# Second product of an MLP on one core: who reads PSUM, and who makes the lower parts of the stationary operands

## The chip, the cores and the metric

The program runs on one core of one Trainium2 chip. The metric is the device time of one execution in microseconds (us). Three runs of the kernel before gave 2746.65, 2749.07 and 2749.72 us; the median, 2749.07 us, is the time before.

The engines are called as in the profile: PE (TensorE, matrix products), PEld (its weight loads), DVE (VectorE), ACT (ScalarE), POOL (GpSimd) and SP (SyncE, which issues most DMAs). Each works through its own queue in order. PE writes its products to PSUM; DVE and ACT read PSUM, and POOL works on SBUF alone in this kernel.

## The reference

One block of a network: two mixers (a long convolution and a gated linear attention), a projection, and an MLP. The change is in the MLP, of which this is the part that matters:

```python
def _sq_relu_mlp(h, w1, w2):
    return jnp.square(jax.nn.relu(h @ w1)) @ w2
...
        x = x + g1 * (jnp.concatenate([y_hy_l, y_gla_l], axis=-1) @ w_out[l])
        h2 = _rms_norm(x, norm_mlp[l]) * (1.0 + sc2) + sh2
        x = x + g2 * _sq_relu_mlp(h2, w_mlp1[l], w_mlp2[l])
...
    return _rms_norm(x, norm_final)
```

Here `x` is 2048 x 1024, `w_mlp1` 1024 x 4096 and `w_mlp2` 4096 x 1024, all float32.

## The kernel before

Both products of the MLP are done with a scheme of seven block products in place of eight (Strassen's, in Winograd's form). Each operand is cut into 2 x 2 blocks, sums of blocks make seven left and seven right operands, and the seven products are added into the four blocks of the result, some of them by continuing in the same PSUM bank. To keep float32 accuracy, each operand is split into an upper part (`hi`, a cast to float32r by ACT) and a lower part (`lo` = operand - `hi`), and each block product is hi*hi + hi*lo + lo*hi: three matmuls for one.

**The first product** runs in two halves of the tokens (`tb` 0 and 1). For each pair of 128 columns `n` it leaves four blocks of squared ReLU outputs and three sums of them (`s1`, `s2`, `s4`; `put`, lines 1385 to 1407) in the DRAM tensor `d_m`. In the second half `n` runs down from 15 to 0, so that the last block that is put is `tb` 1, `n` 0. The sums `s1` and `s2` are made by POOL, the other two by DVE.

**The second product** (lines 1535 to 1653) is where the change works. It has 64 units: for each of 8 quarters `g` of the inner dimension (two blocks of 256 of the 4096 each) it walks over 8 token blocks `t` of 256 tokens. In the tables of this text "unit t of quarter g" is one pass of the loop `for at, (g, t) in enumerate(un)`. The result of all tokens stays in SBUF as `acc` (16 tiles of 128 x 1024, which begin as the residual `x1`).

One unit has seven block products of six matmuls each, called m1 to m7 after their number in the table `PR`. Each matmul is 128x128 by 128x512. PE's order in a unit is m1, m2, then m4 of the unit before ("late4"), m6, m3 of the unit before ("late3"), m5, m7. Three PSUM banks serve a unit: `x` takes m1, then m6, m7 and m4 on top of it, `y` takes m5 and then m3, `z` takes m2. After every product the bank's present sum is added to a block of `acc` (`more`). So PE can't begin m6 before the bank `x` has been read after m1; it can't begin m7 before it has been read after m6, nor late4 before it has been read after m7. Two products (2.7 us of matmuls) lie between in each case.

Seven such reads belong to a unit. Four of them are "direct": DVE adds PSUM to `acc` (line 1575). The other three (m2, late4, late3) go through ACT, which copies PSUM to `tmp` (line 1578), and POOL, which adds `tmp` to `acc` (line 1579).

The stationary operands `u` of a unit come by one DMA of 896 KB (`load_u`, line 1545) into one of two buffers `ur`, and are split operand by operand (`split_u`): ACT casts `uh`, DVE subtracts for `ul` (helper `split`, lines 231 and 232). `uh` and `ul` have one buffer for each of the seven operands, so that the operand of unit t+1 can be made only after PE has used that of unit t; it is needed about one unit later. Operands 4 and 3 are made in their own unit, after late4 and late3 of the unit before. The DMA for unit t+2 waits until the last operand of unit t (number 3) has been split.

Once per quarter the moving operands change. In unit 7 of a quarter and unit 0 of the next `w2_split` makes them: 14 casts `wh` by ACT and 14 subtractions `wl` by DVE (128x512), with 4 sums of blocks on POOL (`sum_b`, lines 1245 and 1247). In unit 1 of each quarter `w2_raw` loads the next two blocks of `w2` (2 DMAs of 1 MB) and lets POOL multiply them by the gate (8 multiplications of 128x512, line 1442) and make four first differences (lines 1443 and 1444).

In the last quarter (g = 7) each unit also finishes the tokens of the unit before: ACT squares (`squares`), POOL makes the factor, DVE scales with `nf` (`finish`, line 1602), and a DMA writes the output.

The framework's scheduler decides the order in which the instructions stand on each engine within small limits; on PE it is the order of the code.

Of the kernel before, what the change touches and what calls it, by code (L numbers as in the profile page):

```python
# [10 lines left out]
F32 = mybir.dt.float32  # L11
# [3 lines left out]
ALU = mybir.AluOpType  # L15
# [3 lines left out]
P = 128  # L19
# [191 lines left out]
def hybrid_block(ctx: ExitStack, tc, a, out, dbg=None):  # L211
    nc = tc.nc
# [5 lines left out]
    dve = nc.vector  # L218
    gps = nc.gpsimd
# [10 lines left out]
    def split(hi, lo, src):  # L230
        nc.scalar.copy(hi, src)  # L231
        dve.tensor_sub(lo, src, hi.bitcast(F32))  # L232
# [20 lines left out]
    def pt(name="ps"):  # L253
        return psp.tile([P, 512], F32, tag="ps", bufs=8, name=name)

    def sb(name, side="left", stack=ctx):
        return stack.enter_context(tc.tile_pool(name=name, bufs=1, side=side, reuse_waits="tile"))
# [971 lines left out]
    PR = {1: (0, 0), 2: (1, 1), 3: (6, 2), 4: (2, 6), 5: (4, 4), 6: (5, 5), 7: (3, 3)}  # L1229
# [48 lines left out]
    with ExitStack() as eo:  # L1278
        op = sb("op", stack=eo)
# [95 lines left out]
    def full(ps, w, m, start):  # L1375
        for kp in range(4):
            prod(ps, w, m, kp, start and kp == 0, kp == 3)
# [6 lines left out]
    cs_ = {}  # L1384

    def put(n, tb, i, j, src, add=None):

        tag, bufs = ("c0", 2) if i == j == 0 else ("c1", 2) if i == j else ("c", 5)
        c = us.tile([P, 512], F32, tag=tag, bufs=bufs, name="c")
        if add is None:  # L1390
            act(c[:], src[:], AF.Relu)
        else:
            dve.tensor_add(c[:], src[:], add[:])
            act(c[:], c[:], AF.Relu)
        act(c[:], c[:], AF.Square)
        cs_[n, i, j] = c
        if (i, j) != (0, 1):
            store(n, tb, {(0, 0): 0, (1, 0): 1, (1, 1): 2}[i, j], c)
            return

        s1, s2, s4 = (us.tile([P, 512], F32, tag="c", bufs=5, name=m) for m in ("s1", "s2", "s4"))
        gps.tensor_tensor(s1[:], c[:], cs_[n, 1, 1][:], op=ALU.add)
        gps.tensor_sub(s2[:], s1[:], cs_[n, 0, 0][:])
        dve.tensor_sub(c[:], cs_[n, 0, 0][:], c[:])
        dve.tensor_sub(s4[:], cs_[n, 1, 0][:], s2[:])
        for slot, t in ((3, c), (4, s1), (5, s2), (6, s4)):
            store(n, tb, slot, t)

    def store(n, tb, slot, c):
        (put_out if tb and n < 1 else dma)(d_m[tb, n, :, :, slot, :], c[:].rearrange("p (q t) -> p q t", q=4))  # L1410
# [26 lines left out]
    def w2_raw(n):  # L1437

        r = w2r[n] = raw_tile()
        dma(r[:, 0:4, :], a["w2"][n])  # L1440
        for q in range(4):
            gps.tensor_mul(r[:, q, :], r[:, q, :], g2b[:, (q // 2) * 512:(q // 2 + 1) * 512])
        gps.tensor_sub(r[:, 4, :], r[:, 3, :], r[:, 0, :])
        gps.tensor_sub(r[:, 3, :], r[:, 2, :], r[:, 3, :])
# [13 lines left out]
    for tb in range(2):  # L1458

        late = None  # L1460
# [6 lines left out]
        for at in range(1, 16):  # L1467
            n = ns[at]
            w, nxt = wops, {}
            x, y = pt(), pt()  # L1470
# [20 lines left out]
            z = pt()  # L1491
# [29 lines left out]
            def late4(n=n, x=x, w=w, tb=tb):  # L1521
                full(x, w, 4, False)
                put(n, tb, 1, 0, x)

            def late3(n=n, y=y, w=w, u2=u2, tb=tb):
                full(y, w, 3, False)
                put(n, tb, 0, 1, y, u2)

            late = (late4, late3)
# [8 lines left out]
    mf = sb("mf", stack=em)  # L1538
    w2s, uts, ops = w2s, {}, {}
# [6 lines left out]

    def split_u(at, m):
        hi, lo = (mf.tile([P, 2, P], F32R, tag=f"{t}{m}", bufs=1, name=t) for t in ("uh", "ul"))
        split(hi[:], lo[:], uts[at][:, :, PR[m][0], :])
        ops[at, m] = (hi, lo)  # L1550

    load_u(0)
# [10 lines left out]
    def full2(ps, at, m, start):  # L1563
        hi, lo = ops.pop((at, m))
        for kb in range(2):
            wh, wl = w2s[m, kb]
            for i, (x_, y_) in enumerate(((hi, wh), (hi, wl), (lo, wh))):
                mm(ps[:], x_[:, kb, :], y_[:], start=start and kb + i == 0, stop=kb == 1 and i == 2,  # L1568
                   skip_group_check=True)

    def more(ps, t, i, j, direct):

        ac = acc[2 * t + i][:, j * 512:(j + 1) * 512]
        if direct:
            dve.tensor_add(ac, ac, ps[:])  # L1575
        else:
            tmp = mf.tile([P, 512], F32, tag="tmp", bufs=4, name="tmp")
            nc.scalar.copy(tmp[:], ps[:])  # L1578
            gps.tensor_add(ac, ac, tmp[:])  # L1579

    def refill(at, m):

        if at < len(un):
            if un[at][1] == 0:
                w2_split(un[at][0], m, (0, 1))
            split_u(at, m)

    def squares(t):
        rs_ = []
        for i in range(2):  # L1590
            ss = mf.tile([P, 4], F32, tag="ss", bufs=4, name="ss")
            for j in range(2):
                tmp = mf.tile([P, 512], F32, tag="tmp", bufs=4, name="tmp")
                act(tmp[:], acc[2 * t + i][:, j * 512:(j + 1) * 512], AF.Square, accum_out=ss[:, j:j + 1])  # L1594
            gps.tensor_add(ss[:, 2:3], ss[:, 0:1], ss[:, 1:2])  # L1595
            rs_.append(rstd_of(mf, ss[:, 2:3], 1, 1.0 / D, "mrs"))
        return rs_
# [7 lines left out]
    late = None  # L1605
    for at, (g, t) in enumerate(un):
        if g == 0:
            for i in range(2):
                dma(acc[2 * t + i][:], d_x1[(2 * t + i) * P:(2 * t + i + 1) * P, :])
        if t == 1 and g < 7:  # L1610
            for kb in range(2):
                w2_raw(2 * g + 2 + kb)
        x, y = pt(), pt()
        full2(x, at, 1, True)
        more(x, t, 0, 0, True)
        refill(at + 1, 1)
        z = pt()
        full2(z, at, 2, True)
        more(z, t, 0, 0, False)
        refill(at + 1, 2)  # L1620
        if late:
            late[0](False)
        refill(at, 4)
        full2(x, at, 6, False)
        more(x, t, 0, 1, True)
        refill(at + 1, 6)
        if late:
            late[1](False)
        refill(at, 3)
        rs_ = squares(t - 1) if g == 7 and t else None  # L1630
        full2(y, at, 5, True)
        more(y, t, 1, 1, True)
        refill(at + 1, 5)
        full2(x, at, 7, False)
        more(x, t, 1, 1, True)
        refill(at + 1, 7)
        if rs_:
            finish(t - 1, rs_)
        if at + 2 < len(un):
            load_u(at + 2)  # L1640

        def late4(direct, at=at, x=x, t=t):
            full2(x, at, 4, False)
            more(x, t, 1, 0, direct)

        def late3(direct, at=at, y=y, t=t):
            full2(y, at, 3, False)
            more(y, t, 0, 1, direct)

        late = (late4, late3)  # L1650
    late[0](True)
    late[1](True)
    finish(7, squares(7))


# [16 lines left out]
```

## Time and profile before

| what | value |
| --- | --- |
| median of three runs | 2749.07 us |
| the profiled execution, its time | 2743.28 us |
| its span in the profile | 2741.5 us |
| mean granted TensorE clock | 0.966 |
| first matmul of the second product starts | 1973.71 us |
| last matmuls of the second product | about 2732 us |

The profile shows one execution. Its page lists the busy time of each engine, the chain of work that ended last, and groups of instructions: line, engine, operation, output<-inputs, shape and count, then busy time, mean duration of one in ns, and the idle time of the engine just before these instructions with what ended it. The timeline lists instructions in order of time: start and length in us, engine, line, operation, and in brackets the idle time before it and what ended that. The stage of the second product, from 1973.7 us on, is 28% of the span.

### The profile page before, as it was taken

The page shows a single profiled execution, that of the slowest core. Times are in us where ns is not written, and L with a number is a line of the kernel's source. Part 1 is how long each engine was busy: PE and PEld are TensorE (multiplying, and loading weights), DVE is VectorE, ACT ScalarE, POOL GpSimd, SP SyncE. Part 2 cuts the span into 40 slices and gives each one's busy share as a digit, 9 for nine tenths or more (in the row PEclk, how much of TensorE's full clock was granted, in tenths as well). Part 3 has the DMA queues.
Part 4 walks back from the last instruction along what each step waited for, and adds up shares of the span by engine and source line. Part 5 has one row for each costly group of instructions (what it writes and reads, how often), then busy time and mean ns, then how long its engine had stood idle before and what let it go on. Part 6 is the DMA issues. An engine that isn't in the chain of part 4 may idle for free. (4 is left out here: it accounts for less than half of the span.)

```text
span 2741.5 us, 37947 instructions
## 1 busy us (share of the span) xinstructions
PE 2512.5 (92%) x13320; PEld 2059.1 (75%) x13320; DVE 1774.2 (65%) x2772; ACT 1253.4 (46%) x2453; POOL 1073.9 (39%) x898
## 2 busy tenths in 40 slices
PE   9899999999998888999899999999698888888887
PEld 5678978897886777788688877888576667666665
DVE  5755366726668777624655547555578887887887
ACT  6463342325226464434555555555443443443354
POOL 2130321223112122332344434444656655646555
PEclk9899999999999899899999999999899999999999
DMA  5425344434448776656454545545552323232323
GB/s 190 152 81 171 117 139 139 143 107 130 157 139 219 221 226 162 216 174 198 154 160 140 161 145 162 162 146 154 191 202 101 109 81 112 98 112 81 112 96 148
DMA packets 298974, 405.02 MB, mean 148 GB/s; under 512 B 23700, under 2 KB 223256, under 8 KB 288672
## 3 DMA queue, kind: packets, MB, share of 16 engines
q1 hardware_dynamic: 292208, 392.38, 45.2%
q10 hardware_dynamic: 6576, 10.23, 1.1%
q8 instruction: 105, 1.72, 0.3%
q14 instruction: 85, 0.70, 0.1%
HBM read 271.92 MB, written 130.62 MB: 147 GB/s over the span
## 5 line engine op out<-in xcount | busy, mean ns | idle before, releaser
L1568 PE MATMUL ps<-wh,uh 128*128 128x512 f32 x896 | 367.6, 411 | 112.0 <-DVE acc L1575 94.2
L232 DVE TENSOR_TENSOR ul<-ur,uh 128x256 fp32r<-128x256 f32 x448 | 356.0, 821 | 121.1 <-ACT uh L231 120.8
L232 DVE TENSOR_TENSOR wl<-raw,wh 128x512 fp32r<-128x512 f32 x329 | 340.8, 1052 | 97.5 <-ACT wh L231 97.4
L1579 POOL TENSOR_TENSOR acc<-acc,tmp 128x512 f32<-128x512 f32 x190 | 268.8, 1430 | 278.5 <-DVE ul L232 130.7
L1568 PE MATMUL ps<-wh,ul 128*128 128x512 f32 x896 | 358.0, 400 | 4.3 <-DVE ul L232 4.3
L1568 PE MATMUL ps<-wl,uh 128*128 128x512 f32 x896 | 358.7, 400 | 0.0
L1373 PE MATMUL ps<-bh,wh 128*128 128x512 f32 x896 | 349.9, 392 | 6.6 <-ACT bh L231 2.8
L1373 PE MATMUL ps<-bl,wh 128*128 128x512 f32 x896 | 351.1, 392 | 4.4 <-DVE bl L232 4.3
L1373 PE MATMUL ps<-bh,wl 128*128 128x512 f32 x896 | 349.2, 390 | 2.7 <-DVE wl L232 2.7
L231 ACT CAST uh<-ur 128x256 fp32r<-128x256 f32 x448 | 170.5, 407 | 348.2 <-PE ps L1568 171.0
L1568 PEld LDWEIGHTS ps<-wh,uh 128*128 128x128 f32 x896 | 174.2, 194 | 184.2 <-ACT uh L231 57.7
L231 ACT CAST wh<-raw 128x512 fp32r<-128x512 f32 x329 | 202.5, 622 | 213.0 <-PE ps L1373 169.5
L1568 PEld LDWEIGHTS ps<-wh,ul 128*128 128x128 f32 x896 | 173.7, 194 | 43.3 <-DVE ul L232 5.0
L1373 PEld LDWEIGHTS ps<-bh,wh 128*128 128x128 f32 x896 | 168.8, 189 | 45.6 <-ACT bh L231 5.1
L1373 PEld LDWEIGHTS ps<-bl,wh 128*128 128x128 f32 x896 | 168.9, 189 | 42.8 <-DVE bl L232 8.3
L1568 PEld LDWEIGHTS ps<-wl,uh 128*128 128x128 f32 x896 | 174.5, 195 | 33.8
L1373 PEld LDWEIGHTS ps<-bh,wl 128*128 128x128 f32 x896 | 168.6, 188 | 38.2 <-DVE wl L232 3.5
L1575 DVE TENSOR_TENSOR acc<-acc,ps 128x512 f32<-128x512 f32 x258 | 174.3, 676 | 14.9 <-PE ps L1568 14.8
L226 PE MATMUL ph<-hth,whi 128*128 128x512 f32 x384 | 150.9, 393 | 0.0
L228 PE MATMUL ph<-hth,wlo 128*128 128x512 f32 x384 | 149.6, 390 | 0.0
L227 PE MATMUL ph<-htl,whi 128*128 128x512 f32 x384 | 149.4, 389 | 0.0
L226 PE MATMUL pv<-whi,hth 128*128 128x264 f32 x512 | 146.6, 287 | 2.9 <-ACT whi L231 2.9
(283 smaller groups left out, 5313.2 us busy)
## 6 DMA issues: line engine op xcount, KB each, us to landing
ur<-d_m SPq DMA_DIRECT2D x64, 896.0 KB, 4.8
raw<-in_w_dram SPq DMA_DIRECT2D x47, 1024.0 KB, 5.7
d_m<-c SPq DMA_DIRECT2D x124, 256.0 KB, 2.6
d_m<-s SPq DMA_DIRECT2D x93, 256.0 KB, 3.1
xt<-in_x_dram SPq DMA_DIRECT2D x32, 512.0 KB, 5.2
mwt<-in_wada_dram SPq DMA_DIRECT2D x64, 256.0 KB, 3.0
raw<-in_wi_vg_dram SPq DMA_DIRECT2D x20, 528.0 KB, 4.9
wada<-in_wada_dram SPq DMA_DIRECT2D x16, 512.0 KB, 7.3
```

Source lines behind the costliest of these rows:

```text
L226: mm(ps, lh, rh, start=first, stop=False)
L227: mm(ps, lh, rl, start=False, stop=False)
L228: mm(ps, ll, rh, start=False, stop=last)
L231: nc.scalar.copy(hi, src)
L232: dve.tensor_sub(lo, src, hi.bitcast(F32))
L1373: mm(ps[:], x_[:, sl], y_[:, j, :], start=start and i == 0, stop=stop and i == 2, skip_group_check=True)
L1568: mm(ps[:], x_[:, kb, :], y_[:], start=start and kb + i == 0, stop=kb == 1 and i == 2, skip_group_check=True)
L1575: dve.tensor_add(ac, ac, ps[:])
L1579: gps.tensor_add(ac, ac, tmp[:])
```

## The change

Three things are changed.

1. In the second product all seven reads of PSUM in a unit are additions by DVE straight into `acc`. The copies by ACT and the additions by POOL (190 of each in the profile) are gone, and with them the choice `direct`.
2. The subtractions for `ul` go to POOL, except those of the first unit (`at` 0), which stay on DVE. The casts `uh` stay on ACT. The split of the moving operands (`wh`, `wl`) stays as it was.
3. In the first product the sums `s1` and `s2` of the last block put (`tb` 1, `n` 0) are made by DVE in place of POOL.

```diff
@@ put
         s1, s2, s4 = (us.tile([P, 512], F32, tag="c", bufs=5, name=m) for m in ("s1", "s2", "s4"))
-        gps.tensor_tensor(s1[:], c[:], cs_[n, 1, 1][:], op=ALU.add)
-        gps.tensor_sub(s2[:], s1[:], cs_[n, 0, 0][:])
+        eng = dve if tb and n < 1 else gps
+        eng.tensor_tensor(s1[:], c[:], cs_[n, 1, 1][:], op=ALU.add)
+        eng.tensor_sub(s2[:], s1[:], cs_[n, 0, 0][:])
@@ split_u
-        split(hi[:], lo[:], uts[at][:, :, PR[m][0], :])
+        src = uts[at][:, :, PR[m][0], :]
+        nc.scalar.copy(hi[:], src)
+        (gps if at else dve).tensor_sub(lo[:], src, hi[:].bitcast(F32))
@@ more
-    def more(ps, t, i, j, direct):
+    def more(ps, t, i, j):
 
         ac = acc[2 * t + i][:, j * 512:(j + 1) * 512]
-        if direct:
-            dve.tensor_add(ac, ac, ps[:])
-        else:
-            tmp = mf.tile([P, 512], F32, tag="tmp", bufs=4, name="tmp")
-            nc.scalar.copy(tmp[:], ps[:])
-            gps.tensor_add(ac, ac, tmp[:])
+        dve.tensor_add(ac, ac, ps[:])
```

The calls of `more`, `late4` and `late3` lose the argument `direct` and are otherwise the same. PE's order is unchanged.

**POOL, unit 1 of a quarter.** In the rows below `raw` is a block of `w2`, `g2b` the gate, `ur` the loaded operands of a unit (each number is one unit). Before, POOL's queue around `w2_raw` (lines 1442 to 1444) has the additions of `tmp`:

```order
L1579 TENSOR_TENSOR acc2_17493<-acc2_17493,tmp_22329 128x512
L1442 TENSOR_TENSOR raw_22293<-raw_22293,g2b_17509 128x512 x4
L1579 TENSOR_TENSOR acc1_17492<-acc1_17492,tmp_22342 128x512
L1443 TENSOR_TENSOR raw_22293<-raw_22293 128x512
L1444 TENSOR_TENSOR raw_22293<-raw_22293 128x512
L1579 TENSOR_TENSOR acc0_17491<-acc0_17491,tmp_22366 128x512
L1442 TENSOR_TENSOR raw_22301<-raw_22301,g2b_17509 128x512 x4
L1443 TENSOR_TENSOR raw_22301<-raw_22301 128x512
L1444 TENSOR_TENSOR raw_22301<-raw_22301 128x512
```

Now, at the same place (the lines of `w2_raw` are 1443 to 1445 in the changed file, and `ul` is line 1552), the subtractions stand there. `ur_21903` belongs to unit 1, `ur_22001` to unit 2 and `ur_22099` to unit 3 of the quarter:

```order
L1552 TENSOR_TENSOR ul_22029<-ur_22001,uh_22028 128x256
L1552 TENSOR_TENSOR ul_22041<-ur_22001,uh_22040 128x256
L1552 TENSOR_TENSOR ul_22052<-ur_21903,uh_22051 128x256
L1443 TENSOR_TENSOR raw_22003<-raw_22003,g2b_17509 128x512 x4
L1552 TENSOR_TENSOR ul_22063<-ur_22001,uh_22062 128x256
L1444 TENSOR_TENSOR raw_22003<-raw_22003 128x512
L1552 TENSOR_TENSOR ul_22074<-ur_21903,uh_22073 128x256
L1445 TENSOR_TENSOR raw_22003<-raw_22003 128x512
L1552 TENSOR_TENSOR ul_22085<-ur_22001,uh_22084 128x256
L1443 TENSOR_TENSOR raw_22011<-raw_22011,g2b_17509 128x512 x4
L1552 TENSOR_TENSOR ul_22096<-ur_22001,uh_22095 128x256
L1444 TENSOR_TENSOR raw_22011<-raw_22011 128x512
```

By the order of the code the seven `ul` here are operands 1 and 2 of unit 2, operand 4 of unit 1, then operand 6 of unit 2, 3 of unit 1, 5 and 7 of unit 2. The last one stands behind all eight multiplications; one more difference (line 1445) follows, and then operand 1 of unit 3.

**DVE, the change of quarters.** `wl` is the lower part of a moving operand, `ps` a PSUM bank. Before, from the first `wl` of unit 7 on:

```order
L232 TENSOR_TENSOR wl_22847<-raw_22293,wh_22846 128x512
L1575 TENSOR_TENSOR acc14_17505<-acc14_17505,ps_22837 128x512
L232 TENSOR_TENSOR wl_22852<-raw_22301,wh_22851 128x512
L232 TENSOR_TENSOR ul_22857<-ur_22835,uh_22856 128x256
L232 TENSOR_TENSOR wl_22871<-raw_22293,wh_22870 128x512
L232 TENSOR_TENSOR wl_22876<-raw_22301,wh_22875 128x512
L232 TENSOR_TENSOR ul_22881<-ur_22835,uh_22880 128x256
L232 TENSOR_TENSOR ul_22894<-ur_22747,uh_22893 128x256
L1575 TENSOR_TENSOR acc14_17505<-acc14_17505,ps_22837 128x512
```

Now the same stretch, with line 1577 for the reads of PSUM:

```order
L232 TENSOR_TENSOR wl_22521<-raw_22003,wh_22520 128x512
L1577 TENSOR_TENSOR acc14_17505<-acc14_17505,ps_22511 128x512
L232 TENSOR_TENSOR wl_22526<-raw_22011,wh_22525 128x512
L1577 TENSOR_TENSOR acc14_17505<-acc14_17505,ps_22534 128x512
L232 TENSOR_TENSOR wl_22543<-raw_22003,wh_22542 128x512
L232 TENSOR_TENSOR wl_22548<-raw_22011,wh_22547 128x512
L1577 TENSOR_TENSOR acc13_17504<-acc13_17504,ps_22429 128x512
L1577 TENSOR_TENSOR acc14_17505<-acc14_17505,ps_22511 128x512
```

Between the reads after m1 and after m6 of unit 7 (the first and the last `acc14` row, bank 22837 before and 22511 now) there stood three `wl` and three `ul`; now there stand three `wl` and two further reads, those after m2 and after late4.

More of the change, by code (lines that the diff above doesn't have):

```diff
@@ L1614, in hybrid_block @@
         full2(x, at, 1, True)
-        more(x, t, 0, 0, True)
+        more(x, t, 0, 0)
         refill(at + 1, 1)
@@ L1618, in hybrid_block @@
         full2(z, at, 2, True)
-        more(z, t, 0, 0, False)
+        more(z, t, 0, 0)
         refill(at + 1, 2)
         if late:
-            late[0](False)
+            late[0]()
         refill(at, 4)
         full2(x, at, 6, False)
-        more(x, t, 0, 1, True)
+        more(x, t, 0, 1)
         refill(at + 1, 6)
         if late:
-            late[1](False)
+            late[1]()
         refill(at, 3)
@@ L1631, in hybrid_block @@
         full2(y, at, 5, True)
-        more(y, t, 1, 1, True)
+        more(y, t, 1, 1)
         refill(at + 1, 5)
         full2(x, at, 7, False)
-        more(x, t, 1, 1, True)
+        more(x, t, 1, 1)
         refill(at + 1, 7)
@@ L1640, in hybrid_block, with late4, late3 @@
             load_u(at + 2)
-        def late4(direct, at=at, x=x, t=t):
+        def late4(at=at, x=x, t=t):
             full2(x, at, 4, False)
-            more(x, t, 1, 0, direct)
-        def late3(direct, at=at, y=y, t=t):
+            more(x, t, 1, 0)
+        def late3(at=at, y=y, t=t):
             full2(y, at, 3, False)
-            more(y, t, 0, 1, direct)
+            more(y, t, 0, 1)
         late = (late4, late3)
-    late[0](True)
-    late[1](True)
+    late[0]()
+    late[1]()
     finish(7, squares(7))
```

## The prediction

> **What bounds the kernel now.** I read the page first, for the stage and its waits, then PE's timeline, then DVE's and POOL's at the places where PE stops.
>
> ```profile
> span 2741.5 us, 37947 instructions
> ...
> L1568 PE MATMUL ps<-wh,uh 128*128 128x512 f32 x896 | 367.6, 411 | 112.0 <-DVE acc L1575 94.2
> L232 DVE TENSOR_TENSOR ul<-ur,uh 128x256 fp32r<-128x256 f32 x448 | 356.0, 821 | 121.1 <-ACT uh L231 120.8
> ...
> L1579 POOL TENSOR_TENSOR acc<-acc,tmp 128x512 f32<-128x512 f32 x190 | 268.8, 1430 | 278.5 <-DVE ul L232 130.7
> ...
> L1575 DVE TENSOR_TENSOR acc<-acc,ps 128x512 f32<-128x512 f32 x258 | 174.3, 676 | 14.9 <-PE ps L1568 14.8
> ```
>
> PE waits 94 us for DVE's reads of PSUM, though a read takes only 676 ns. DVE is late because of what stands ahead in its queue: `ul`, 821 ns in the mean. PE's timeline shows what it could do and where it stops.
>
> ```profile
> 2301.21 0.39 PE L1568 MATMUL ps<-wh,ul 128*128 128x512 f32 x1
> 2301.44 0.39 PE L1568 MATMUL ps<-wh,uh 128*128 128x512 f32 x1
> ...
> 2246.47 0.39 PE L1568 MATMUL ps<-wh,ul 128*128 128x512 f32 x1
> 2251.07 0.77 PE L1568 MATMUL ps<-wh,uh 128*128 128x512 f32 x1 [4.22 <-DVE acc L1575]
> 2251.64 0.63 PE L1568 MATMUL ps<-wl,uh 128*128 128x512 f32 x1
> 2252.07 0.63 PE L1568 MATMUL ps<-wh,ul 128*128 128x512 f32 x1
> ...
> 2281.97 0.80 PE L1568 MATMUL ps<-wh,uh 128*128 128x512 f32 x1 [3.00 <-DVE acc L1575]
> 2311.21 0.47 PE L1568 MATMUL ps<-wh,uh 128*128 128x512 f32 x1 [0.77 <-DVE acc L1575]
> 2321.92 0.47 PE L1568 MATMUL ps<-wh,uh 128*128 128x512 f32 x1 [0.91 <-DVE acc L1575]
> 2341.88 0.39 PE L1568 MATMUL ps<-wh,ul 128*128 128x512 f32 x1
> 2346.48 0.77 PE L1568 MATMUL ps<-wh,uh 128*128 128x512 f32 x1 [4.22 <-DVE acc L1575]
> 2730.07 0.50 PE L1568 MATMUL ps<-wh,uh 128*128 128x512 f32 x1 [1.91 <-DVE acc L1575]
> ```
>
> Undisturbed, a matmul follows the last after 0.227 us (the first two rows), so a unit of 42 takes 9.52 us. From 2246.47 to 2341.88, one quarter of 8 units (336 matmuls), pass 95.4 us; 336 x 0.2266 are 76.1. **A quarter loses 19.3 us**: waits of 4.22 us (change of quarters) and 3.00 us (after `w2_raw`), about 1 us in each quiet unit, and slow matmuls after the long waits. After 4.22 us they follow at 0.43 us (2251.64 to 2252.07); the window below has the granted clock behind the 3.00 us wait.
>
> ```profile
> 2278.00:2288.00 10.00, 7.00 (x26) 5.37 (x25) 7.98 (x10) 2.90 (x8) 9.84 (x9) 0.83 0.29 92
> 2288.00:2298.00 10.00, 8.82 (x38) 6.64 (x37) 8.29 (x12) 2.13 (x6) 6.85 (x5) 1.00 0.29 93
> ```
>
> The column after the five engines is the clock: 0.83, then 1.00. PE's timeline has about 13 matmuls, each 0.2 us longer, after either wait: 2.6 us more. After 1.91 us (the 2730.07 row) there is no such run. Starts of all matmuls, summed over the stage, give the losses: 7.6 us at its start, 3.7 in the first seven units, 115.1 in six full quarters, 7.7 at the last change, 15.3 in the last quarter: 149 us.
>
> **What the change takes away.** Why is `ul` slow?
>
> ```profile
> 2303.31 0.41 DVE L232 TENSOR_TENSOR ul<-ur,uh 128x256 fp32r<-128x256 f32 x1
> 2308.90 4.14 POOL L1579 TENSOR_TENSOR acc<-acc,tmp 128x512 f32<-128x512 f32 x3 [6.40 <-DVE ul L232]
> 2309.15 1.31 DVE L232 TENSOR_TENSOR ul<-ur,uh 128x256 fp32r<-128x256 f32 x1 [0.34 <-ACT uh L231]
> 2310.39 0.68 DVE L1575 TENSOR_TENSOR acc<-acc,ps 128x512 f32<-128x512 f32 x1
> ...
> L1575 DVE TENSOR_TENSOR acc<-acc,ps x258: 672/675/689, 1986.2 to 2732.2; 128x512 f32<-128x512 f32 x129
> ```
>
> With POOL idle `ul` takes 0.41 us; beside POOL's addition 1.31, as long as POOL's own. The read of PSUM takes 672 to 689 ns in all 258 cases, with or without POOL. Here the read (2310.39) stands behind that `ul`, and PE stops until 2311.21. In a quiet unit the change leaves DVE seven reads, 7 x 0.676 = 4.7 of 9.52 us, with nothing ahead of them, and two products (2.7 us) as cover for each. **The 1 us of each quiet unit goes.** ACT loses 190 copies that nobody waits long for: nothing. What is late next in a quiet unit? A `ul` on POOL has about 8 us from PE's last use of its buffer to its next, and POOL 5.1 us of work in 9.52. The DMA of `ur` for unit t+2 now waits for POOL's `ul` of operand 3 (7.0 to 7.75 of unit t), lands 4.8 us later, at 3.5 of unit t+1, and is needed at 9.5: six us of cover for what is behind it in SP's queue too.
>
> **What it adds on POOL.** 441 subtractions of 128x256. POOL's nearest rows:
>
> ```profile
> L317 POOL TENSOR_TENSOR glg<-glg,gt 128x256 f32<-128x256 f32 x4 | 2.9, 729 | 17.5 <-ACT gt L315 17.5
> L696 POOL TENSOR_TENSOR st<-st,gnb 128x232 f32<-128x232 f32 x16 | 12.4, 778 | 35.3 <-ACT st L695 35.3
> ...
> 2271.53 5.25 POOL L1442 TENSOR_TENSOR raw<-raw,g2b 128x512 f32<-128x512 f32 x4
> 2282.40 5.38 POOL L1442 TENSOR_TENSOR raw<-raw,g2b 128x512 f32<-128x512 f32 x4
> 2287.86 1.35 POOL L1443 TENSOR_TENSOR raw<-raw 128x512 f32<-128x512 f32 x1
> ```
>
> The same shape took 0.73 us; by the 128x232 row it would be 0.86. The output is float32r, which no POOL row has; the ends are 0.73 and 1.43 (the mean of 128x512 above), and I take 0.73, by the row of its own shape. Per quarter POOL has 56 x 0.73 = 41, plus 16 operations on `raw` at 1.3 to 1.35 = 21: 62 of 76 us. It fits, but not evenly.
>
> The Trainium skill, "GPSIMD Engine Reference", section "Engine selection", says that additions of two tensors belong on VectorE, GpSimd being about 2x slower. The trace agrees (0.73 against 0.41 alone), but not beside POOL, where DVE's 1.31 is the slower. By the rule alone 441 x 0.32 = 141 us of engine time are added; that costs time only if POOL becomes the bound, which is the second rival.
>
> *Unit 1, `w2_raw`.* By the order, POOL does operand 4 of unit 1, then 4 multiplications, one `ul`, a difference, `ul`, a difference, `ul`, 4 multiplications, `ul` (operand 7 of unit 2), 2 differences, `ul` (operand 1 of unit 3). When do the first begin? The DMAs:
>
> ```profile
> ur<-d_m SPq DMA_DIRECT2D x64, 896.0 KB, 4.8
> raw<-in_w_dram SPq DMA_DIRECT2D x47, 1024.0 KB, 5.7
> ```
>
> Let 0 be unit 1's start. Operand 3 of unit 0 is split after late3 there, about -1.5; `ur` of unit 2 is issued then and lands at about 3.8 (4.8 us, some more beside `raw`); `raw` is issued at -1 and lands at 4.7. Three `ul` end at 6.5. Then 4 x 1.29 to 11.7, `ul`, difference, `ul`, difference, `ul` to 16.45, multiplications to 21.6, operand 7 of unit 2 at 22.35. PE's third matmul of m7 wants it at 9.52 + 8.16 + 0.45 = 18.1. **PE waits 4.2 us**, pays 2.6 for the clock, and about 0.8 for operand 1 of unit 3 (25.7): 7.6 us. The earlier `ul` are just in time (operand 5: 16.45 against 16.8). If `ur` lands so early that only late4 sets the start, all is 1.5 us earlier; at 0.86 it is 0.9 later: 4 to 9 us.
>
> *Change of quarters.* In unit 7 DVE has 10 `wl` and 7 reads, POOL 7 `ul` and 4 sums.
>
> ```profile
> 2257.62 0.68 DVE L232 TENSOR_TENSOR wl<-raw,wh 128x512 fp32r<-128x512 f32 x1
> 1968.10 9.66 DVE L232 TENSOR_TENSOR wl<-raw,wh 128x512 fp32r<-128x512 f32 x7 [5.70 <-ACT wh L231]
> ```
>
> A `wl` takes 0.68 us alone, 1.38 (9.66 / 7) where POOL is always busy. I let a `wl` (0.65 at the pace of the queue) and an instruction of POOL take turns, and reads run beside POOL. With 0 at the start of unit 7, DVE's order then gives: `wl` to 2.2, read after m1 to 2.85; POOL's first sum holds the second `wl` until 3.55, so to 4.2; read after m2 to 4.85; `wl` to 5.6; second sum; `wl` 6.9 to 7.55; reads after late4 and m6 to 8.9, where PE wants m7 at 8.16 (0.85 late with the read's end and a hand-over). Four more `wl`, each behind one `ul` or sum, and two reads put the read after m7 at 15.65, where late4 wants it at 13.1 (2.6 late); two more `wl` put the read after m1 of unit 0 at 18.5, where m6 wants it at 17.05 (1.5 late). **5.0 us**, in pieces too short for the clock; 1 us with `wl` at 0.75, 7 and the 2.6 at 1.38. Before, seven `ul` stood in the same queue, and the pieces were the 4.22 us, its clock and some 1.6 us behind it. The four `wl` of unit 0 and its seven reads (some 9 us) fit into 9.52, so the lag is caught up there.
>
> *The ends.* At the stage's start `ul` of unit 0 stay on DVE, but POOL's multiplications now come behind POOL's `ul`, so fewer collide:
>
> ```profile
> 1977.68 5.99 DVE L232 TENSOR_TENSOR ul<-ur,uh 128x256 fp32r<-128x256 f32 x8
> 1979.21 0.80 PE L1568 MATMUL ps<-wh,ul 128*128 128x512 f32 x1 [4.28 <-DVE ul L232]
> 1958.57 1.26 POOL L1402 TENSOR_TENSOR s<-c 128x512 f32<-128x512 f32 x1 [1.43 <-ACT c L1395]
> 1959.91 1.77 POOL L1403 TENSOR_TENSOR s<-s,c 128x512 f32<-128x512 f32 x1
> ```
>
> I take 3.6 of the 7.6 us there. The last sums by DVE take 2 x 0.69 for 1.26 + 1.77: 1 us less (0 to 1.7; transfers may cover it). In the last quarter DVE's scaling (1.28 us, twice) still stands ahead of reads: 12 of 15.3 stay. First units: 1 for `w2_raw`, 1 for the rest, of 3.7.
>
> **The sum.** Losses after: 4 + 2 + 6 x (5.0 + 7.6) + 5 + 12 = 98.6 against 149.4, and 1 us of the sums: 52 us less. 2743.3 - 52 = 2691 for an execution like the profiled one; that one was 5.8 us below the median, so **2697 us**.
>
> **Rivals.**
> 1. *POOL keeps up* (chance 0.14): `w2_raw` makes no long wait, since `raw` and `ur` come earlier or multiplications end sooner. Quarters lose 6 us: 6 x 6.6 = 40 us less than the forecast, 2657. For it: the estimated waits are few us on a chain of 16. Against: 17 us of POOL's work stand in one piece.
> 2. *POOL becomes the bound*, and the time is slower (0.15). It needs no wait by itself: at x us per `ul` POOL's quarter takes 21.5 + 56x, and the old 95.4 us are reached at 1.32. With the pieces of POOL's queue in the way break-even comes at about 1.05 already: operand 7 is 2.2 us later, the wait 6.4, and recovery, 1.05 against PE's 1.36 us a product, is too slow to be free before the change. At 1.43 a quarter takes 101.6 us: 6 x 6.2 = 37 us more, some 2786 against the median. For it: float32r output without a row, two-part reads. Against: 729 ns.
> 3. *One wait takes the place of another* (0.16): `ul` at 0.86 to 1.05, or `wl` at 1.38; quarters lose 16 to 19 us, gain 5 to 30, 2720 to 2744. The part below 5.5 us counts as no change.
>
> **How the numbers follow.** The forecast (gain 30 to 75) has 0.55. About 0.2% (5.5 us) is what a measurement here tells from no change. Faster: 0.55 + 0.14 + 0.09 of the third rival = 0.78; same: its other 0.07 and 0.01 of the second = 0.08; slower: the remaining 0.14 of the second. The range leaves out the slow rival and the far end of the first: 2655 to 2746.
>
> **What would show it.** PE's waits for DVE reads should vanish from quiet units, whose period falls to 9.5 us; a wait for POOL's `ul` should appear in unit 2 of each quarter at m7, with a clock of about 0.85 behind it; pieces of waits for DVE remain around unit 7. `ul` on POOL should show 0.73 to 0.87 us, and `acc` on DVE 0.676. I am wrong if `ul` takes over 1 us, or if the 5 us at the change of quarters are 10.

## The result, and the profile after

| | before | after |
| --- | --- | --- |
| median of four runs | 2749.39 us (2746.65 to 2752.69) | 2707.41 us (2705.73 to 2709.86) |
| ratio to before, 95% interval | | 0.9848 [0.983, 0.9865] |
| the profiled execution, its time | 2743.28 us | 2706.48 us |
| mean granted TensorE clock | 0.966 | 0.963 |

The changed kernel is 42 us (1.5%) faster by the medians; forecast were 52. The page of after, groups by line (busy us, mean ns, then idle time ahead and what ended it):

```profile
span 2704.7 us, 37929 instructions
...
L1577 DVE TENSOR_TENSOR acc<-acc,ps 128x512 f32<-128x512 f32 x448 | 304.8, 685 | 263.9 <-PE ps L1571 256.8
L1552 POOL TENSOR_TENSOR ul<-ur,uh 128x256 fp32r<-128x256 f32 x441 | 350.1, 823 | 187.2 <-ACT uh L1551 172.2
L1571 PE MATMUL ps<-wh,uh 128*128 128x512 f32 x896 | 362.7, 405 | 59.2 <-DVE acc L1577 40.1
...
L1571 PE MATMUL ps<-wh,ul 128*128 128x512 f32 x896 | 361.3, 403 | 24.4 <-POOL ul L1552 24.2
L1551 ACT CAST uh<-ur 128x256 fp32r<-128x256 f32 x448 | 163.4, 404 | 471.4 <-DMA ur<-d_m 261.3
```

PE's wait for DVE's reads has fallen from 94.2 to 40.1 us, a wait for POOL's `ul` has come (24.2), and DVE now waits for PE (256.8 us). The last row became the most telling one: ACT stands 261.3 us waiting for the load of `ur`. Before it stood 167.0 there.

What PE loses in the stage against its undisturbed pace (0.2266 us from matmul to matmul), worked out from the starts of all its matmuls as in the prediction; "per quarter" is the mean of six full quarters. The first product (m1) of unit 1 is counted with the change of quarters, since slow matmuls behind the last stop of unit 0 run on into it; cut at the end of unit 0, the two rows of after would be 7.6 and 7.5:

| place | before | forecast | after |
| --- | --- | --- | --- |
| start of the stage and first units | 10.7 | 6 | 5.5 |
| change of quarters (units 7 and 0), per quarter | 7.5 | 5.0 | 8.2 (5.8 to 10.7) |
| units 1 to 3 (`w2_raw`), per quarter | 8.5 | 7.6 | 6.9 |
| units 4 to 6, per quarter | 3.2 | 0 | 0.0 |
| last change | 7.7 | 5 | 5.8 |
| last quarter | 15.4 | 12 | 7.0 |
| sum | 148.8 | 98.6 | 108.9 |

The first row and the sum of before are 0.6 below the prediction's 11.3 and 149.4, since three rows of PE's timeline hold two matmuls each (x2). So the stage is 39.9 us shorter; the pause between the two products is 1.0 us shorter (17.66 before, 16.68 now, from last to first matmul), and the unchanged code ahead of it ended 4.0 us later in this execution. 39.9 + 1.0 - 4.0 = 36.9, beside 36.8 between the profiled times. In all the profiles below that unchanged code ends between 1956 and 1972 us, so single executions differ by that much for no reason in the change, and I compare losses of the stage first and medians second.

**A quiet unit.** DVE's timeline in unit 4 of a quarter (start, length, and in brackets the idle time before it):

```profile
2290.77 0.69 DVE L1577 TENSOR_TENSOR acc<-acc,ps 128x512 f32<-128x512 f32 x1 [0.67 <-PE ps L1571]
2292.13 0.69 DVE L1577 TENSOR_TENSOR acc<-acc,ps 128x512 f32<-128x512 f32 x1 [0.67 <-PE ps L1571]
```

A read every 1.36 us, the length of a product, with DVE idle half of the time: PE sets the pace.

**After `w2_raw`.** POOL's timeline, then PE's two stops behind it:

```profile
2271.50 5.04 POOL L1443 TENSOR_TENSOR raw<-raw,g2b 128x512 f32<-128x512 f32 x4
2276.48 0.74 POOL L1552 TENSOR_TENSOR ul<-ur,uh 128x256 fp32r<-128x256 f32 x1
2277.16 1.30 POOL L1444 TENSOR_TENSOR raw<-raw 128x512 f32<-128x512 f32 x1
2278.54 1.27 POOL L1445 TENSOR_TENSOR raw<-raw 128x512 f32<-128x512 f32 x1
2279.78 4.84 POOL L1552 TENSOR_TENSOR ul<-ur,uh 128x256 fp32r<-128x256 f32 x7
...
2277.27 0.50 PE L1571 MATMUL ps<-wh,ul 128*128 128x512 f32 x1 [2.35 <-POOL ul L1552]
2280.55 0.80 PE L1571 MATMUL ps<-wh,ul 128*128 128x512 f32 x1 [1.32 <-POOL ul L1552]
```

PE waits at m7 of unit 2 for the `ul` that stands behind all eight multiplications, and for operand 1 of unit 3 behind two more differences: the wait that the prediction named.

**The change of quarters.** PE's stops at the longest of them, then the chain behind the last stop, on POOL, SP, ACT and DVE:

```profile
2235.99 0.47 PE L1571 MATMUL ps<-wh,uh 128*128 128x512 f32 x1 [1.02 <-DVE acc L1577]
2242.40 0.47 PE L1571 MATMUL ps<-wh,uh 128*128 128x512 f32 x1 [2.07 <-DVE acc L1577]
2244.75 0.47 PE L1571 MATMUL ps<-wh,uh 128*128 128x512 f32 x1 [0.73 <-DVE acc L1577]
2252.72 0.77 PE L1571 MATMUL ps<-wh,uh 128*128 128x512 f32 x1 [3.63 <-DVE acc L1577]
...
2237.60 3.51 POOL L1247 TENSOR_TENSOR raw<-raw 128x512 f32<-128x512 f32 x2
2241.07 4.22 POOL L1552 TENSOR_TENSOR ul<-ur,uh 128x256 fp32r<-128x256 f32 x4
...
2243.48 0.36 SPq L1546 DMA_DIRECT2D ur<-d_m  x1
...
2248.33 0.71 ACT L1551 CAST uh<-ur 128x256 fp32r<-128x256 f32 x2 [8.87 <-DMA ur<-d_m]
2248.95 0.61 ACT L231 CAST wh<-raw 128x512 fp32r<-128x512 f32 x1
...
2249.60 1.18 DVE L232 TENSOR_TENSOR wl<-raw,wh 128x512 fp32r<-128x512 f32 x1 [4.20 <-ACT wh L231]
2250.70 0.68 DVE L1577 TENSOR_TENSOR acc<-acc,ps 128x512 f32<-128x512 f32 x1
```

Read it from the bottom. PE waits 3.63 us for a read of PSUM (2250.70) that takes 0.68. The read stands behind a `wl`, which waited 4.20 us for its `wh`; that cast stood on ACT behind two casts `uh`, for which ACT had waited 8.87 us: the load of `ur` for unit 1 had not landed. It was issued at 2243.48, just when the second of the four `ul` at 2241.07 ends (they take over 1 us each there, between DVE's `wl`), and these stood behind two sums of blocks, 3.51 us. A page that says "PE waits for DVE" thus hides a load that waits for POOL. This stop, at m7 of unit 0, is not among the three that the prediction names.

### The profile page after: what moved, and what is told of

It reads as the page before. It is cut to its first block, busy times and chain, and to the rows that moved or that the text cites. A ratio compares the mean times of both kernels' runs of the same rounds, so it can differ in the third digit from the quotient of the medians.

```text
span 2704.7 us, 37929 instructions
## 1 busy us (share of the span) xinstructions
PE 2506.1 (93%) x13320; PEld 2065.8 (76%) x13320; DVE 1576.1 (58%) x2523; ACT 1161.1 (43%) x2263; POOL 1150.6 (43%) x1147
## 4 chain that ended last, share of the span: by engine, by line
PE 39%; DVE 6%; POOL 6%; DMA 3%; issue 3%; ACT 1%; ACTq 0%; POOLq 0%; SPq 0%; DVEq 0%
PE ps L1373 20%; PE ps L1571 14%; DVE wl L232 2%; POOL raw L1443 2%; POOL ul L1552 2%; DMA ur<-d_m 2%; PE po L228 2%; PE po L227 2%; PE po L226 2%; DVE acc L1577 1%; DVE bl L232 1%; DMA raw<-in_w_out_dram 0%; ACT wh L231 0%; DVE acc L1600 0%; POOL ss L1593 0%
## 5 line engine op out<-in xcount | busy, mean ns | idle before, releaser
L1577 DVE TENSOR_TENSOR acc<-acc,ps 128x512 f32<-128x512 f32 x448 | 304.8, 685 | 263.9 <-PE ps L1571 256.8
L1552 POOL TENSOR_TENSOR ul<-ur,uh 128x256 fp32r<-128x256 f32 x441 | 350.1, 823 | 187.2 <-ACT uh L1551 172.2
L1571 PE MATMUL ps<-wh,uh 128*128 128x512 f32 x896 | 362.7, 405 | 59.2 <-DVE acc L1577 40.1
L1571 PE MATMUL ps<-wh,ul 128*128 128x512 f32 x896 | 361.3, 403 | 24.4 <-POOL ul L1552 24.2
L1551 ACT CAST uh<-ur 128x256 fp32r<-128x256 f32 x448 | 163.4, 404 | 471.4 <-DMA ur<-d_m 261.3
L228 PE MATMUL ph<-hth,wlo 128*128 128x512 f32 x384 | 149.4, 389 | 0.0
L227 PE MATMUL ph<-htl,whi 128*128 128x512 f32 x384 | 149.4, 389 | 0.0
L227 PE MATMUL pv<-wlo,hth 128*128 128x264 f32 x512 | 145.6, 285 | 0.6 <-DVE wlo L232 0.6
```

Of the source, the lines that this page charges most:

```text
L227: mm(ps, lh, rl, start=False, stop=False)
L228: mm(ps, ll, rh, start=False, stop=last)
L1551: nc.scalar.copy(hi[:], src)
L1552: (gps if at else dve).tensor_sub(lo[:], src, hi[:].bitcast(F32))
```

## The experiments

The runs were to tell apart what each part of the change is worth, and where the two remaining losses of a quarter come from: POOL's `ul` themselves, the block of `w2_raw` on POOL, or the late load of `ur`. What each theory says of a run stands in its expectation. Losses of a run are "change / units 1 to 3 / units 4 to 6" per full quarter, with after at 8.2 / 6.9 / 0.0.

**1. `ul` back on DVE, the reads all on DVE** (run twice, once with a single run, once in three rounds):

```diff
-        (gps if at else dve).tensor_sub(lo[:], src, hi[:].bitcast(F32))
+        dve.tensor_sub(lo[:], src, hi[:].bitcast(F32))
```

> The changed kernel with all lower parts `ul` made by DVE again, all seven reads of PSUM still by DVE. Theory A (the reads were late because `ul` stood ahead of them in DVE's queue and was held up by POOL's additions; without those additions `ul` takes 0.41 us): DVE has 7 x (0.676 + 0.41) = 7.6 of 9.52 us, quiet units lose 0 to 0.3 us each, and what is lost at `w2_raw` and at the change of quarters is of the size of the changed kernel's: 2700 to 2730 us, and no wait of PE for POOL. Theory B (it is the move of `ul` to POOL that brings the gain, because DVE's queue is too full with both): quiet units lose about 1 us as before, 2740 us or more.

> The kernel with all `ul` on DVE and all reads on DVE once more, for an interval. Theory A: 2675 to 2688 us, ratio to the kernel before 0.972 to 0.977, clearly under the changed kernel's 0.9848: the move of `ul` to POOL costs about 20 us. Rival (the single run was a lucky one): 0.980 to 0.987.

2681.74 us, then 2674.65 us, ratio 0.9725 [0.971, 0.974]; losses of the second 3.6 / 6.9 / 0.0, 80.0 in all. With `ul` and all reads on DVE, PE still runs through the quiet units without a stop. In the page of the second run:

```profile
L1552 DVE TENSOR_TENSOR ul<-ur,uh 128x256 fp32r<-128x256 f32 x448 | 251.1, 574 | 17.5 <-ACT uh L1551 17.0
```

With POOL's additions gone, `ul` on DVE falls from 821 to 574 ns by itself. So the reads, with the sums of the third part (about 1 us), bring 0.0275 of the time (75 us), and the second part of the change, `ul` on POOL, gives 0.0123 (34 us) back. Theory A holds on what made the reads late, and B falls; the time lies under A's 2700 to 2730, since the change of quarters lost 3.6 us and not the 8.2 of after. ACT waits 94.1 us for the load of `ur` in the second run, beside 261.3 in after.

**2. `ul` on POOL, but three reads of seven by ACT and POOL as before** (m2, late4 and late3):

```diff
+        if direct:
+            dve.tensor_add(ac, ac, ps[:])
+        else:
+            tmp = mf.tile([P, 512], F32, tag="tmp", bufs=4, name="tmp")
+            nc.scalar.copy(tmp[:], ps[:])
+            gps.tensor_add(ac, ac, tmp[:])
```

> The changed kernel with three of seven reads through a copy by ACT and an addition by POOL again, `ul` still on POOL. Theory A (POOL becomes the bound): per quarter POOL has 56 x 0.73 + 24 x 1.29 + 21.5 = 93.5 us against 91.2 us that a quarter of the changed kernel takes, so quarters take 95 to 100 us and the time is 2740 to 2800 us, with POOL's share over 90% in quiet stretches. Theory C (the way of the reads does not matter once `ul` has left DVE): 2700 to 2715 us.

2885.67 us: far slower than expected, with losses of 20.4 / 13.0 / 2.9. POOL's work alone doesn't explain that, since POOL was busy for only 338.76 of 400 us (85%, 2200 to 2600 us), where theory A had over 90%. Its page points to another cause, the load (the last number is ACT's wait for it):

```profile
L1551 ACT CAST uh<-ur 128x256 fp32r<-128x256 f32 x448 | 168.5, 409 | 542.4 <-DMA ur<-d_m 392.3
```

A version of this kernel with earlier loads was not tried, so for this one the cause is argued, not shown.

**3. The last sums by POOL again:** `eng = gps`.

> The changed kernel with the last `s1` and `s2` made by POOL again. The pause of PE between the two products was 17.66 us before (1956.05 to 1973.71) and 16.68 us in the changed kernel. If the sums are the cause, the pause here is 17.4 to 17.9 us and the time about 1 us longer, which one run can't tell; if the pause is set by transfers or by DVE's other work, it stays at 16.5 to 16.9 us.

2713.16 us in one run. The pause between the products is 18.1 us (1967.17 to 1985.27) beside 16.68, a little over the expected 17.4 to 17.9. All profiles together say about 1 us: three kernels with these sums on POOL have pauses of 17.1 to 18.1 us, eleven with the sums on DVE 16.4 to 16.9.

**4. Each `ul` on POOL half as long again** (the first half of it is written a second time with the same values):

```diff
+        if at:
+            gps.tensor_sub(lo[:, :, 0:64], src[:, :, 0:64], hi[:, :, 0:64].bitcast(F32))
```

> The changed kernel with each `ul` of POOL followed by a second subtraction of half its size (the same values again), so that an operand costs POOL 0.73 + about 0.45 = 1.18 us. The prediction put the break-even with the kernel before at about 1.05 us: by it quarters take 96 to 100 us and the time is 2750 to 2785 us. Rival: POOL's sum alone counts, 56 x 1.18 + 21.5 = 87.6 us per quarter, which is under 91.2: waits at `w2_raw` grow by 7 x 0.45 = 3 us per quarter and no more, about 2730 us.

2843.92 us, losses 18.9 / 8.6 / 4.7: again much worse than POOL's sum, with POOL idle for a sixth of the time. Both expectations missed. A loop through the load would do that: a late `ul` delays the issue of a load that takes 4.8 us, and POOL then waits for that load. Run 11 tests it.

**5. `w2_raw` spread:** its 12 operations stand two to a unit in units 1 to 6.

```diff
-            for kb in range(2):
-                w2_raw(2 * g + 2 + kb)
+            steps = iter([s for kb in range(2) for s in w2_steps(2 * g + 2 + kb)])
...
+        step()
...
+        step()
```

(`w2_steps` gives the same four multiplications and two differences of `w2_raw` as a list; `step` issues the next one, ahead of m6's and of m7's place in the code.)

> The changed kernel with the twelve operations of `w2_raw` on POOL spread over units 1 to 6 of a quarter, two in each, in place of one piece in unit 1. Theory A (the piece of 17 us keeps POOL's `ul` waiting, 6.2 to 7.4 us per quarter in units 1 to 3): these units lose 0 to 1.5 us, the time is 2663 to 2680 us, and the wait of PE for `ul` in unit 2 is gone. Rival (POOL has too little room, 62 of 76 us, so that the waits only move to later units): 2695 us or more.

2687.05 us, ratio 0.9771 [0.9756, 0.9785]; losses 11.5 / 0.2 / 0.0. Units 1 to 3 lose nothing, so POOL's block was their loss. But the change of quarters lost 3.3 us more in the mean, so the time missed the range. The stop at m7 of unit 7 has grown in every change (1.34 to 4.58 us, before the spread at most 1.02), and the one at m7 of unit 0 is 3.06 to 3.73 us throughout (0.79 to 3.65 in after). In the third change, the one shown above, the first and the last of its four stops are:

```profile
2233.23 0.47 PE L1571 MATMUL ps<-wh,uh 128*128 128x512 f32 x1 [1.93 <-DVE acc L1577]
...
2249.80 0.76 PE L1571 MATMUL ps<-wh,uh 128*128 128x512 f32 x1 [3.49 <-DVE acc L1577]
```

**6. A third buffer for `ur`:**

```diff
-        uts[at] = mf.tile([P, 2, 7, P], F32, tag="ur", bufs=2, name="ur")
+        uts[at] = mf.tile([P, 2, 7, P], F32, tag="ur", bufs=3, name="ur")
```

> The changed kernel with three buffers `ur` in place of two, so that a DMA of operands need not wait for POOL's last `ul` two units back. Theory D (at the change of quarters POOL is late, the DMA for unit 1 is issued late, ACT's queue stands on its `uh`, and the casts `wh`, then `wl`, then DVE's reads stand behind it): units 7 and 0 lose 5 us in place of 5.8 to 10.7, 2680 to 2698 us. Rival (the waits there come from DVE's own queue): as the changed kernel, 2702 to 2712 us.

2671.34 us, ratio 0.9711 [0.9697, 0.9726]; losses 2.4 / 7.6 / 0.0. ACT no longer waits for the load anywhere, and theory D holds: of 8.2 us at the change of quarters the load made 5.8. The gain is larger than expected (2680 to 2698).

**7. The spread with `ul` on DVE.**

> All `ul` and all reads on DVE, and `w2_raw` spread over units 1 to 6. Theory A: in the kernel with `ul` on DVE units 1 to 3 lose 7.2 to 8.9 us because twelve operations of POOL in one piece each hold a `ul` up; two per unit hold up two `ul` by about 1 us each, which DVE's 7.6 of 9.52 us leave room for: units 1 to 3 lose 0 to 2 us, 2640 to 2655 us. Rival (each hold-up is passed on to PE, 0.5 to 1 us in all six units): 2670 to 2690 us.

2671.87 us, ratio 0.9714 [0.9688, 0.974]. It doesn't answer its question. With `ul` on DVE nothing else stands in POOL's queue in these units, so the operations still run four and two in a row; losses are 3.0 / 6.4 / 0.0, nearly as without the edit.

**8. Spread and third buffer together.**

> Both remaining losses of the changed kernel taken together: a third buffer `ur` (alone: 2671 us, change of quarters 2.4 us) and POOL's 12 operations of `w2_raw` spread two per unit over units 1 to 6 (alone: 2687 us, units 1 to 3 at 0 to 0.7 us, change of quarters 9 to 14 us). Theory (what the spread lost at the change was the load of `ur` issued late, which a third buffer makes harmless): per full quarter 2.4 at the change and 0 to 1 in units 1 to 3, so the stage loses about 30 us in place of 109, and the time is 2620 to 2640. Rival (the spread lost there because POOL's own work, the sums of blocks and `ul`, comes late in units 7 and 0): change of quarters stays at 6 us or more, 2655 to 2680.

2631.42 us, ratio 0.9565 [0.955, 0.9579]: the fastest kernel of the study, 76 us below after, inside the range of the theory. Losses 3.2 / 0.0 / 0.0, 31.8 in the whole stage. These are all of PE's stops of over 0.2 us in a full quarter, with the first two of the next (2296.48 on):

```profile
2217.16 0.47 PE L1571 MATMUL ps<-wh,uh 128*128 128x512 f32 x1 [1.52 <-DVE acc L1577]
2219.51 0.47 PE L1571 MATMUL ps<-wh,uh 128*128 128x512 f32 x1 [0.73 <-DVE acc L1577]
...
2296.48 0.47 PE L1571 MATMUL ps<-wh,uh 128*128 128x512 f32 x1 [1.49 <-DVE acc L1577]
2298.82 0.47 PE L1571 MATMUL ps<-wh,uh 128*128 128x512 f32 x1 [0.71 <-DVE acc L1577]
```

From 2217.16 to 2296.48 pass 79.3 us, and 76.1 of them are matmuls. What the spread alone lost at the change was the load. The two edits together save more than their sum (36 and 20 us from after).

**9. Third buffer with `ul` on DVE.**

> `ul` back on DVE, all reads of PSUM by DVE, and a third buffer `ur`. If the third buffer helps only where POOL makes `ul` late, nothing changes against the two buffers with `ul` on DVE (2674.65 us): 2665 to 2680, change of quarters 3 to 4.5 us, units 1 to 3 at 7 to 9. Rival (the load is exposed there too): the change of quarters falls to about 1 us, 2650 to 2660. Beside the run with `ul` on POOL and three buffers (2671 us) it tells whether the place of `ul` matters at all once the load is early.

2650.17 us, ratio 0.964 [0.962, 0.9661]; losses 3.0 / 2.6 / 0.0. The rival has the time, but not the place: the change of quarters stays (3.6 with two buffers), and units 1 to 3 fall from 6.9 to 2.6. Beside run 6 (`ul` on POOL, three buffers, 0.9711) the intervals don't meet: `ul` on POOL costs 0.0071 (20 us) even with early loads.

**10. The kernel before with a third buffer.**

> The kernel before with a third buffer `ur` and nothing else. Theory (before, DVE's queue was late, not the load): no change, 2743 to 2755, about 19 us lost in each quarter. Rival (the load was late before as well, and the third buffer is worth as much there as after the change, 36 us): 2710 to 2720.

2689.23 us (2683.12 to 2698.61), ratio 0.9778 [0.9752, 0.9804]. **The theory is wrong, and so was my reading of before**: the load was late there too, and one number in one line is worth more (61 us) than the whole change (42). Losses 7.5 / 0.2 / 1.8. These are all of PE's stops of over 0.5 us between 2200 and 2340 us; there are two places in a quarter, m7 of unit 7 (2248.77, 2334.53) and, shorter, in unit 4:

```profile
2209.39 0.47 PE L1568 MATMUL ps<-wh,uh 128*128 128x512 f32 x1 [1.20 <-DVE acc L1575]
2248.77 0.76 PE L1568 MATMUL ps<-wh,uh 128*128 128x512 f32 x1 [4.85 <-DVE acc L1575]
2295.11 0.47 PE L1568 MATMUL ps<-wh,uh 128*128 128x512 f32 x1 [1.43 <-DVE acc L1575]
2334.53 0.47 PE L1568 MATMUL ps<-wh,uh 128*128 128x512 f32 x1 [4.85 <-DVE acc L1575]
```

The 4.2 us stop of the change of quarters is still there (4.85); the 3.00 us stop behind `w2_raw` has vanished. Its cause can be read in the trace of before, on SP, ACT and DVE ahead of that stop (which is at 2281.97):

```profile
2266.64 0.34 SPq L1440 DMA_DIRECT2D raw<-in_w_dram  x1
2267.08 0.39 SPq L1545 DMA_DIRECT2D ur<-d_m  x1
2267.59 0.38 SPq L1440 DMA_DIRECT2D raw<-in_w_dram  x1
...
2273.68 1.03 ACT L231 CAST uh<-ur 128x256 fp32r<-128x256 f32 x3 [2.17 <-DMA ur<-d_m]
...
2274.11 5.79 DVE L232 TENSOR_TENSOR ul<-ur,uh 128x256 fp32r<-128x256 f32 x4 [1.23 <-ACT uh L231]
2279.83 0.68 DVE L1575 TENSOR_TENSOR acc<-acc,ps 128x512 f32<-128x512 f32 x1
```

The load stands between the two loads of `raw` and lands 6.6 us after its issue. Four `ul` then come at once, beside POOL's multiplications (2271.53 in the prediction's rows), and take 5.79 us in place of the 1.64 that four take alone; the read behind them is late. With a third buffer the same `ul` come one by one.

**11. The longer `ul` of run 4, with a third buffer.**

> `ul` on POOL lengthened by half (0.77 + 0.51 us), now with a third buffer `ur`; with two buffers this took 2844 us, though POOL was busy for 83% of the stage. Theory (the excess is the load that a late `ul` of POOL holds back): with a third buffer about 10 us are lost at the change of quarters and 10 to 14 in units 1 to 3, 2710 to 2760. Rival (POOL itself is the bound at this length): 2800 to 2845 again.

2741.83 us in one run, losses 4.1 / 13.7 / 0.0: as the theory said in time and in units 1 to 3, and less than its 10 us at the change. The windows of both runs over the same stretch (busy time of PE, PEld, DVE, ACT and POOL, each with its count; clock; share of the DMA engines; GB/s), first with two buffers, then with three:

```profile
2200.00:2600.00 400.00, 322.65 (x1268) 248.97 (x1268) 185.39 (x257) 93.58 (x253) 330.54 (x478) 0.93 0.27 91
...
2200.00:2600.00 400.00, 351.30 (x1454) 281.73 (x1453) 215.26 (x298) 126.48 (x298) 383.06 (x553) 0.93 0.31 102
```

POOL goes from 330.54 to 383.06 us (83 to 96%): with two buffers it stood and waited for loads that it had itself delayed. 102 us of the 2844 lay in this loop, by one run of each; only with three buffers is POOL near its bound.

The main runs side by side, medians in us:

| | two buffers `ur` | three |
| --- | --- | --- |
| kernel before | 2749 | 2689 |
| all reads by DVE, `ul` by DVE | 2675 | 2650 |
| after: all reads by DVE, `ul` by POOL | 2707 | 2671 |
| after, with `w2_raw` spread | 2687 | 2631 |

A spread version with `ul` on DVE that really spreads was not made, so whether POOL is the better place for `ul` in the best kernel stays open.

## Why the prediction was right, and where it was wrong

- **"The 1 us of each quiet unit goes": right in the number, and half right in the reason.** 3.2 us per quarter in units 4 to 6 became 0.0. The loss needed two things at once: `ul` beside POOL's additions ahead of the reads, as the prediction says, and a load that came late, which it doesn't say. In before ACT waits for the load in these units too, just ahead of the prediction's rows from 2308.90 on, so that the `ul` behind it come in a bunch:

```profile
2307.62 0.71 ACT L231 CAST uh<-ur 128x256 fp32r<-128x256 f32 x2 [5.12 <-DMA ur<-d_m]
```

  Run 1 takes away POOL's additions and keeps two buffers, and these units lose nothing. Run 10 keeps the additions and `ul` on DVE and takes away the late load, and units 5 and 6 lose nothing either (under 0.1 us); its 1.8 us all lie in unit 4, behind eight additions that POOL has put off for `w2_raw` (11.13 us in one piece from 2288.68).
- **`ul` on POOL takes 0.73 us: right** (median 0.742). The mean is 0.823: the 85 instances beside DVE's `wl` take 1.10 in the mean and up to 1.29, and six beside the scaling of the last quarter 1.71.
- **`w2_raw`, 7.6 us: right**, 6.9 measured, at m7 of unit 2 (2.35 to 3.97 us, forecast 4.2) and at operand 1 of unit 3 as worked out. The spread, which takes away POOL's block alone, brings it to 0.2. That the old loss of 8.5 us at this place had another cause, a load between two others, I had not seen; old and new loss are nearly equal by chance.
- **Change of quarters, 5.0 us: the step that failed.** Measured 8.2. Its three stops are there: m7 of unit 7 up to 1.02 us (forecast 0.85), late4 1.52 to 2.10 (2.6), m6 of unit 0 0.57 to 0.74 (1.5). The forecast let DVE's `wl` take turns with POOL; without late loads all stops there sum to 2.4 us (run 6), so that part was too dear by half. What is missing is the load, 5.8 us, above all the stop at m7 of unit 0 (0.79 to 3.65 us), which run 6 doesn't have. The sentence that failed is "six us of cover for what is behind it in SP's queue too". It counted the time until PE needs the operand, in a quiet unit. Two things were left out: that operand 3's `ul` stands behind POOL's sums in unit 7, which delays the issue; and that ACT serves its queue in order, so that a cast `uh` without data holds up the casts `wh` behind it, on which `wl` and DVE's reads hang. In the quiet units of after the same lateness is free, as ACT's timeline shows, where nothing else stands in its queue and PE loses nothing:

```profile
2296.86 1.38 ACT L1551 CAST uh<-ur 128x256 fp32r<-128x256 f32 x4 [4.49 <-DMA ur<-d_m]
```

- **"In pieces too short for the clock": not always.** In five of the seven changes 7 to 12 matmuls at half clock follow, 1.4 to 2.4 us; the two without are the two of 5.8.
- **Ends of the stage:** start and first units 5.5 for 6; last quarter 7.0 for 12, where I had left nearly all of the old loss standing. The sums were worth about 1 us as forecast.
- **The sum.** 98.6 forecast, 108.9 measured: the changes of quarters are 20 us above (6 x 3.2 and 0.8), the rest 10 below, so part of the nearness of the sum is luck. The sum for before, 149.4, was 0.6 too high: its 3.7 for the first seven units is 3.0. The forecast of 2691 for an execution like the profiled one, plus these 10.3 and 4.0 for the unchanged code ahead, is 2705, beside 2706.48.
- **The rivals.** POOL never became the bound at 0.74 us per `ul`. But its break-even, 1.05 us, was set too high: with `ul` at 1.28 us in two instructions (775 and 507 ns) the kernel is at 2844 us, 94 above before, though POOL's own sum of 21.5 + 56 x 1.28 = 93 us fits into the old 95.4 of a quarter. A straight line between -42 us at 0.74 and +94 at 1.28 puts break-even at about 0.91, an estimate. With a third buffer the same `ul` give 2742.
- **The rule on where additions belong** was put aside for POOL's 0.73 against DVE's 1.31 in the prediction. The trace says otherwise: DVE's 1.31 was caused by the additions on POOL that the same change removes. The Trainium skill, "GPSIMD Engine Reference", section "Engine selection", which places additions of two tensors on VectorE, is borne out here by runs 1 and 9: 34 us with two buffers, 20 with three.

## What to carry to other kernels

When an engine waits for another one, follow the chain to its end before you move work: here "PE waits for DVE" ended in three places at a load whose buffer came free late (behind `w2_raw` and in quiet units of before, at the change of quarters of after), and a third buffer alone was worth more than the change. A cast that waits for its data holds up all that stands behind it in its engine's queue, so a load's cover is to be counted to the first instruction behind it that anyone needs, in the busiest unit, not to its own consumer in a quiet one. Price the parts of a change apart: the price of an instruction (`ul`, 1.31 us) may be made by the neighbour that another part of the change removes.

## What the runs showed of the hardware

- **The half clock doesn't go by the length of one wait, but by how it lies on a grid of 3.41 us.** Two changes of quarters in after. First PE's timeline at the earlier one, then windows around both, cut at points of that grid (busy time of PE, PEld, DVE, ACT and POOL with their counts, clock, share of the DMA engines, GB/s):

```profile
2150.83 0.47 PE L1571 MATMUL ps<-wh,uh 128*128 128x512 f32 x1 [1.94 <-DVE acc L1577]
...
2152.06 0.54 PE L1571 MATMUL ps<-wh,ul 128*128 128x512 f32 x1
2153.17 0.77 PE L1571 MATMUL ps<-wh,uh 128*128 128x512 f32 x1 [0.58 <-DVE acc L1577]
2153.74 0.63 PE L1571 MATMUL ps<-wl,uh 128*128 128x512 f32 x1
2154.16 0.63 PE L1571 MATMUL ps<-wh,ul 128*128 128x512 f32 x1
...
2148.74:2152.15 3.41, 1.47 (x7) 1.05 (x6) 3.41 (x4) 0.00 (x0) 3.41 (x4) 1.00 0.00 0
2152.15:2155.56 3.41, 2.83 (x8) 1.96 (x7) 1.56 (x3) 0.00 (x0) 1.55 (x2) 0.50 0.71 227
...
2240.90:2244.32 3.42, 1.61 (x6) 1.05 (x6) 3.42 (x5) 0.00 (x0) 3.42 (x4) 1.00 0.00 0
2244.32:2247.73 3.41, 2.98 (x13) 2.52 (x14) 0.97 (x2) 0.00 (x0) 0.97 (x2) 1.00 0.80 269
```

  After waits of 1.94 and 0.58 us matmuls follow at 0.43 us, 12 of them; after 2.07 and 0.73 us (2242.40 and 2244.75, above) they follow at 0.23. In each of the 14 traces the granted clock changes only at points that lie a multiple of 3.41 us apart. The stretch up to 2152.15 has the wait of 1.94 us nearly whole, PE is busy for 1.47 us of it, and the next stretch runs at 0.50. The wait of 2.07 us is cut by such a point, the stretch up to 2244.32 still has 1.61 us of busy PE, and the clock stays at 1.00. Counted from 1985 us on in all 14 traces: of the 133 such stretches at full clock in which PE had no matmul running for more than 1.92 us, all were followed by half clock, and of 2545 others two. The Trainium skill, "TensorE: Matmul & The Clock Gate", section "What's actually happening", puts the half clock after at least one idle window of some 3.4 us. The trace agrees with the length of the window, but the one above was busy for 1.47 us of it, so by the measurement a window that is idle for little more than half is enough.

- **Reads of PSUM don't mind POOL, subtractions in SBUF do.** The answers on the reads and on `ul` in after (minimum, median, maximum in ns):

```profile
L1577 DVE TENSOR_TENSOR acc<-acc,ps x448: 672/687/691, 1980.1 to 2695.4; 128x512 f32<-128x512 f32 x150
...
L1552 POOL TENSOR_TENSOR ul<-ur,uh x441: 719/742/1712, 1980.2 to 2688.9; 128x256 fp32r<-128x256 f32 x147
```

  The Trainium skill, "SBUF — State Buffer", section "Who interferes with whom", says that a DVE instruction with two inputs in SBUF contends with a GpSimd instruction that reads SBUF, and that one with at most one such input doesn't, outside the 2-port performance modes. The trace agrees: `acc` (one input from PSUM) keeps to 672 to 691 ns whatever POOL does, while `ul` and `wl` lengthen each other: beside POOL `wl` takes 1.02 us in the mean in this stage, alone 0.68 (9 cases), and `ul` beside `wl` the 1.10 named above.
